# A split QKV projection on one core: a row tile of x loaded from ScalarE's queue, a block of w cut into slices, and a cast given to ScalarE

## The chip, the core and the metric

The kernel runs on one core of a Trainium2 chip. TensorE (PE) multiplies, VectorE (DVE), ScalarE (ACT) and GpSimd (POOL) cast, add and copy, and DMA queues that SyncE (SP) or ScalarE start move data between HBM and SBUF. The metric is the device time of one execution in microseconds; lower is better. Before the change it was 358.88 us, the median of 3 runs (358.77 to 358.99).

## The reference

```python
batch, seq, hidden = 16, 512, 768          # x (16, 512, 768), w_qkv (768, 2304), float32
qkv = np.matmul(x, w_qkv)
q, k, v = qkv[..., :768], qkv[..., 768:1536], qkv[..., 1536:]
return np.stack([q, k, v], axis=0).astype(np.float32)
```

So one matrix of 8192 x 768 is multiplied by one of 768 x 2304, and the result is stored as three matrices of 8192 x 768.

## The kernel before

**Tiling.** The 8192 rows of x are taken in 32 pairs of two row tiles of 128 rows. The contraction of 768 is cut into six steps j of 128. The 2304 columns of w are two groups of 1024 columns (q = 0 and q = 1 in the code, each of two blocks of 512, c = 0 and 1) and 256 remainder columns between them. From the third pair on (p = 2) a pair is multiplied by a group with a scheme of seven products instead of eight: `product` (L236) makes them from sums of row tiles (`sums_x`, L207) and sums of blocks of w (`sum_w`, L111, on VectorE). Two of the seven take bf16 copies (`xb`, `b1`), the other five take fp32r tiles (`s`, `t`, and `b22`, a copy of the lower half of block 1 that GpSimd makes). The remainder columns are multiplied plainly in bf16 (`rem`, L315, with the weights `w_rem0` and `w_rem1`).

**The start.** While w still arrives, pairs 0 and 1 are multiplied plainly with bf16 blocks (`block`, L468): block 0 of group 0 (24 matmuls, six steps j by four row tiles), then block 1 of group 0 (24 more), then the remainder columns of pairs 0 and 1 (24 matmuls of 256 columns, one `rem` per pair). Then comes the first product of pair 2 with group 0 (`do(u, 1)`, L580), and after it the third pair's other products are mixed with block work on group 1. After about 60 us the kernel is in a regular loop over pairs.

**The order is written out by hand.** `tc.manual_schedule()` keeps every engine's instructions in the order of the code, so one that waits holds all behind it on its engine. What matters here, by engine:

- SyncE's queue (L442 to L451): pair 0, pair 1, six slices of block 0, block 1 as two halves of three slices (0 to 2 and 3 to 5, 768 KB each), the remainder columns `str` (768 KB), pair 2 as eight DMAs of 96 KB (`load_x_rows`, four for each row tile), then the first block of group 1. Each DMA issue waits for the eighth DMA before it to have landed, since eight semaphores go round.
- VectorE (L547 to L563): cast of slice 0 and 2 of block 1, `sum_w(0, 1)`, cast of slice 4, `sum_w(0, 2)`, the cast into `w_rem0` (L558), then the two transposes of pair 2's row tiles (`transpose`, L155).
- ScalarE (L548 to L570): cast of slice 1, of 3 and of 5 of block 1, between and behind them the copies out of PSUM (`late0`, then `late`, L476), then `round_row(2, 0, act)` (L203), the bf16 copy of pair 2's first row tile that `do(u, 1)` multiplies.
- GpSimd (L559, L560): the cast into `w_rem1`, which waits for `str`; behind it the cast into `b22`, which reads slices 3 to 5 of block 1.

Of the kernel before, what the change touches and what calls it, by code (L numbers as in the profile page):

```python
# [10 lines left out]
def kernel(  # L11
# [20 lines left out]
    nc = tc.nc  # L32
    P = 128
    G = 32
# [4 lines left out]
    KT = K // P  # L39
    KH = KT // 2  # L40
    KC = K // 4
    NP = M // (2 * P)
    CB = 512
    REM = N3 - 4 * CB
    Q_OFF = (0, 2 * CB + REM)
    R_OFF = 2 * CB
    fp32 = mybir.dt.float32
    f32r = mybir.dt.float32r
    bf16 = mybir.dt.bfloat16
    ident = mybir.ActivationFunctionType.Identity  # L50
# [11 lines left out]
    o_pool = ctx.enter_context(tc.tile_pool(name="o", bufs=5))  # L62
# [13 lines left out]
    w_rem = [w_pool.tile([P, KH, REM], bf16, name="w_rem0"), None]  # L76
# [13 lines left out]
    def load_w(dst, j0, nj, off, cols):  # L90
        rows = w_qkv.rearrange("(p j) n -> p j n", j=KT)
        nc.sync.dma_start(dst, rows[:, j0:j0 + nj, off:off + cols])  # L92

    stage = {}

    def load_blocks(q, c, nj=KH):
        if q == 0:
            t = tq_pool.tile([P, KT, CB], fp32, name="st0", tag="tq")
            for j in range(0, KT, nj):
                load_w(t[:, j:j + nj], j, nj, Q_OFF[q] + c * CB, CB)  # L100
            stage[q, 0, c], stage[q, 1, c] = t[:, :KH, :], t[:, KH:, :]
        else:
            for h in range(2):
                if c == 0 and h == 0:
                    t = st_first
                else:
                    t = st_pool.tile([P, KH, CB], fp32, name="st1", tag="st")[:]
                load_w(t, h * KH, KH, Q_OFF[q] + c * CB, CB)
                stage[q, h, c] = t
# [11 lines left out]
    xin, xf, xb, sr = {}, {}, {}, {}  # L121
# [5 lines left out]
        for i in (2 * h, 2 * h + 1):  # L127
            eng.dma_start(xin[p][i * G:(i + 1) * G], rows[:, :, i * KC:(i + 1) * KC])

    def load_x_rows(p, parts=range(8)):  # L130
        if p not in xin:
            xin[p] = xin_pool.tile([P, 2 * P // G, KC], fp32, name="xin")
        rows = x_flat[p * 2 * P:(p + 1) * 2 * P, :].rearrange("(g b) k -> b g k", b=G)
        for n in parts:
            r, i = divmod(n, 4)
            gs = slice(r * P // G, (r + 1) * P // G)
            nc.sync.dma_start(  # L137
                xin[p][i * G:(i + 1) * G, gs], rows[:, gs, i * KC:(i + 1) * KC]
            )

# [18 lines left out]
    def load_rows(p):  # L159
        xin[p] = xin_pool.tile([P, 2, K], fp32, name="xin")  # L160
        rows = x_flat[p * 2 * P:(p + 1) * 2 * P, :]
        nc.sync.dma_start(xin[p][:], rows.rearrange("(r m) k -> m r k", m=P))  # L162
# [21 lines left out]
    def copy_row(p, r, h, eng):  # L184
        n = slice(h * KH, (h + 1) * KH)
        dst, src = xb[p][:, n, r * P:(r + 1) * P], turned_rows[p, r][:, n, :]
        if eng is nc.scalar:
            eng.activation(dst, src, ident)
        else:
            eng.tensor_copy(out=dst, in_=src)  # L190
# [5 lines left out]
    act, dve = nc.scalar, nc.vector  # L196
# [32 lines left out]
    def quad(p, q, pool=o_pool, tag="o"):  # L229
        u = Quad()  # L230
        u.p, u.q = p, q
        u.o = pool.tile([P, 2, 2 * CB], fp32, name="o", tag=tag)
        u.x = u.y = u.z = None
        return u
# [208 lines left out]
    nc.scalar.activation(tiny[:], zero[:, :1], ident)  # L443
    make_identity(nc, eye)
    load_rows(1)
    load_blocks(0, 0, 1)
    load_blocks(0, 1)
    st_rem = o_pool.tile([P, KT, REM], fp32, name="str", tag="o")
    load_w(st_rem[:], 0, KT, R_OFF, REM)
    load_x_rows(2)  # L450
    load_blocks(1, 0)  # L451

    def busy(n):

# [4 lines left out]
    def cast_j(q, c, w, j, eng=act):  # L459
        src = stage[q, j // KH, c][:, j % KH, :]  # L460
        if eng is act:
            eng.activation(w[:, j, :], src, ident)
        else:
            eng.tensor_copy(out=w[:, j, :], in_=src)
# [76 lines left out]
    shared_cast(b1[0][:, 1], stage[0, 0, 0][:, 1, :], 320)  # L541
    for p, r in ((0, 0), (0, 1), (1, 0), (1, 1)):
        copy_row(p, r, 1, act)
    for j in range(2, KT):
        cast_j(0, 0, b1[0], j, dve)
    late0 = block(0, 0, b1[0], singles)
# [9 lines left out]
    for f in late0[1:]:  # L556
        f()
    dve.tensor_copy(out=w_rem[0][:], in_=st_rem[:, :KH])  # L558
    nc.gpsimd.tensor_copy(out=w_rem[1][:], in_=st_rem[:, KH:])  # L559
    nc.gpsimd.tensor_copy(out=b22[0][:], in_=stage[0, 1, 1])  # L560
    late = block(0, 1, bt, [((j, ), range(4)) for j in range(KT)])
    rems = [rem(p) for p in range(2)]
# [20 lines left out]
    load_blocks(1, 1)  # L583
    for store in rem_stores:
        store()
    load_x_rows(3)
    for p in range(2):
        store_quad(quads[p, 0])
    load_x(4, nc.sync)
# [62 lines left out]
    for p in range(ND + 3, NP - 1, 2):  # L652
# [16 lines left out]
        c, d = quad(p + 1, 0), quad(p + 1, 1)  # L669
# [34 lines left out]
```

## Time and profile before

| what | value |
|---|---|
| median of 3 runs | 358.88 us (358.77 to 358.99) |
| the profiled execution's own time | 358.8 us |
| its span, first to last instruction | 357.0 us |
| TensorE busy | 350.5 us, 98% of the span |
| VectorE, ScalarE, GpSimd busy | 74%, 52%, 50% |
| DMA | 108.10 MB, mean 303 GB/s |
| granted TensorE clock | 1.000 |

A time in the profile is in us from the start of the span. A line of the timeline gives start, length, engine, source line, operation, the tile written and the tile read, their shapes and how many instructions are merged into the line; a bracket at its end says how long the engine sat idle before it and what ended that. A view by stretches gives, for each stretch of the span, the busy time of PE, PEld (weight loads), DVE, ACT and POOL, then the granted clock, the DMA engines' busy share and what they moved in GB/s. PE's matmuls are pipelined, so a start is a surer mark than an end, and a matmul that is listed with 379 ns may follow the one before it by far less.

### The profile page before, as it was taken

The page shows a single profiled execution, that of the slowest core. Times are in us where ns is not written, and L with a number is a line of the kernel's source. Part 1 is how long each engine was busy: PE and PEld are TensorE (multiplying, and loading weights), DVE is VectorE, ACT ScalarE, POOL GpSimd, SP SyncE. Part 2 cuts the span into 40 slices and gives each one's busy share as a digit, 9 for nine tenths or more (in the row PEclk, how much of TensorE's full clock was granted, in tenths as well). Part 3 has the DMA queues.
Part 4 walks back from the last instruction along what each step waited for, and adds up shares of the span by engine and source line. Part 5 has one row for each costly group of instructions (what it writes and reads, how often), then busy time and mean ns, then how long its engine had stood idle before and what let it go on. Part 6 is the DMA issues. An engine that isn't in the chain of part 4 may idle for free.

```text
span 357.0 us, 5317 instructions
## 1 busy us (share of the span) xinstructions
PE 350.5 (98%) x1757; PEld 252.0 (71%) x1776; DVE 264.5 (74%) x309; ACT 186.0 (52%) x320; POOL 177.6 (50%) x184
## 2 busy tenths in 40 slices
PE   8999999999999999999999999999999999999996
PEld 3464677768677686877768777686877768677674
DVE  3799876796877869777695877869777695876743
ACT  5588654545454553645545454553645545454553
POOL 0121774276566453665535566353665535566320
PEclk9999999999999999999999999999999999999999
DMA  7998999999999898999979899798999989896497
GB/s 301 375 351 273 322 369 356 381 302 372 259 345 310 256 355 206 355 258 299 352 188 388 226 328 320 237 376 213 347 263 308 329 213 376 231 328 249 155 376 264
DMA packets 82075, 108.10 MB, mean 303 GB/s; under 512 B 4992, under 2 KB 62080, under 8 KB 82048
## 3 DMA queue, kind: packets, MB, share of 16 engines
q1 hardware_dynamic: 75088, 102.52, 85.8%
q10 hardware_dynamic: 6960, 5.24, 5.6%
q8 instruction: 14, 0.23, 0.3%
q14 instruction: 13, 0.11, 0.1%
HBM read 32.24 MB, written 75.50 MB: 302 GB/s over the span
## 4 chain that ended last, share of the span: by engine, by line
PE 70%; POOL 15%; DVE 6%; DMA 4%; issue 3%; SPq 1%; ACT 0%; DVEq 0%
PE ps L247 56%; PE ps L310 11%; DVE xf L155 6%; POOL xb L194 5%; POOL s L215 3%; POOL s L214 3%; POOL s L216 3%; PE ps L484 3%; DMA xin<-in_x_dram 2%; DMA st<-in_w_qkv_dram 2%; SPq L137 1%; SPq L162 0%; ACT xb L203 0%; DVE o L293 0%; SPq L92 0%
## 5 line engine op out<-in xcount | busy, mean ns | idle before, releaser
L247 PE MATMUL ps<-t,s 128*128 128x512 f32 x720 | 177.9, 395 | 0.0
L247 PEld LDWEIGHTS ps<-t,s 128*128 128x128 f32 x720 | 135.0, 188 | 29.5
L155 DVE STREAM_TRANSPOSE xf<-xin 128x768 f32<-128x768 f32 (+1 forms) x45 | 93.3, 2075 | 2.2 <-DMA xin<-in_x_dram 2.2
L247 PE MATMUL ps<-b,xb 128*128 128x512 bf16 x343 | 81.5, 379 | 1.4 <-ACT xb L203 0.3
L287 DVE TENSOR_TENSOR o<-o,ps 128x512 f32<-128x512 f32 x56 | 38.5, 688 | 52.5 <-ACT o L286 52.5
L194 POOL CAST xb<-xf 128x1536 bf16<-128x1536 f32 x28 | 41.1, 1468 | 57.8 <-DVE xf L155 57.8
L214 POOL TENSOR_TENSOR s<-xf 128x384 fp32r<-128x384 f32 x29 | 31.0, 1069 | 72.1 <-DVE xf L155 70.3
L247 PEld LDWEIGHTS <-xb 128*128 128x128 bf16 x360 | 33.9, 98 | 37.0 <-issue 4.2
L293 DVE TENSOR_TENSOR o<-o,ps 128x512 f32<-128x512 f32 x60 | 41.1, 687 | 20.5 <-PE ps L247 19.4
L286 ACT ACTIVATE o<-ps 128x512 f32<-128x512 f32 x56 | 33.5, 598 | 42.0 <-PE ps L247 42.0
L247 PE MATMUL ps<-b,s 128*128 128x512 f32 x180 | 50.5, 389 | 0.0
L290 ACT ACTIVATE o<-ps 128x512 f32<-128x512 f32 x60 | 35.9, 599 | 25.2 <-PE ps L247 22.8
L367 DVE TENSOR_TENSOR o<-o,ps 128x512 f32<-128x512 f32 x78 | 47.8, 682 | 0.0
L310 PE MATMUL ps<-w_rem,xb 128*128 128x256 bf16 x384 | 47.3, 273 | 0.0
L275 ACT ACTIVATE o<-ps 128x512 f32<-128x512 f32 x60 | 36.0, 601 | 19.4 <-PE ps L247 14.1
L310 PEld LDWEIGHTS <-xb 128*128 128x128 bf16 x384 | 37.4, 98 | 11.4 <-issue 0.8
L324 ACT ACTIVATE orem<-ps 128x512 f32<-128x512 f32 x31 | 18.5, 597 | 47.6 <-PE ps L310 34.0
L247 PEld LDWEIGHTS ps<-b,s 128*128 128x128 f32 x180 | 33.8, 188 | 7.1
L215 POOL TENSOR_TENSOR s<-s,xf 128x384 fp32r<-128x384 f32 x29 | 29.6, 1021 | 2.3
L216 POOL TENSOR_TENSOR s<-xf 128x384 fp32r<-128x384 f32 x29 | 29.5, 1017 | 0.0
L218 POOL TENSOR_TENSOR s<-xf,s 128x384 fp32r<-128x384 f32 x29 | 29.4, 1012 | 0.0
L371 ACT ACTIVATE o<-ps 128x512 f32<-128x512 f32 x26 | 15.6, 599 | 17.8 <-PE ps L247 17.2
(51 smaller groups left out, 162.6 us busy)
## 6 DMA issues: line engine op xcount, KB each, us to landing
out_dram<-o SPq DMA_DIRECT2D x60, 768.0 KB, 4.6
out_dram<-o SPq DMA_DIRECT2D x75, 256.0 KB, 3.8
xin<-in_x_dram SPq DMA_DIRECT2D x88, 192.0 KB, 5.7
out_dram<-orem SPq DMA_DIRECT2D x31, 256.0 KB, 2.4
xin<-in_x_dram ACTq DMA_DIRECT2D x24, 192.0 KB, 4.1
st<-in_w_qkv_dram SPq DMA_DIRECT2D x5, 768.0 KB, 7.7
xin<-in_x_dram SPq DMA_DIRECT2D x2, 768.0 KB, 4.9
st<-in_w_qkv_dram SPq DMA_DIRECT2D x6, 256.0 KB, 5.9
```

The costliest lines, as they stand in the source:

```text
L155: nc.vector.transpose(turned[:, g:g + n], rows[:, g:g + n])
L194: nc.gpsimd.tensor_copy(out=xb[p][:], in_=xf[p][:])
L214: 1: lambda g: g.tensor_tensor(s[:, 1], a21, a22, op=add),
L215: 2: lambda g: g.tensor_tensor(s[:, 2], s[:, 1], a11, op=sub),
L216: 3: lambda g: g.tensor_tensor(s[:, 3], a11, a21, op=sub),
L247: nc.tensor.matmul(ps[:], lhs[j], rhs[j], start=(start and j == 0), stop=(j == KH - 1), skip_group_check=True,)
L275: nc.scalar.activation(c12, u.x[:], ident)
L287: nc.vector.tensor_tensor(c22, c22, u.y[:], op=add)
L290: nc.scalar.activation(c21, u.x[:], ident)
L293: nc.vector.tensor_tensor(c12, c12, u.y[:], op=add)
L310: nc.tensor.matmul(ps, xb[p][:, j, r * P:(r + 1) * P], w_rem[j // KH][:, j % KH, :], start=(j == 0), stop=(j == KT - 1), skip_group_check= ...
L367: dve.tensor_tensor(c, c, u.z[:], op=add)
```

## The change

Three things are done at once. First, pair 2's first row tile (four DMAs of 96 KB) is issued from ScalarE's queue instead of SyncE's, right behind the copies of pairs 0 and 1's transposed rows; on SyncE's queue the four for the second row tile stay, behind the remainder columns, and all x rows of a tile now go in the order 0, 2, 1, 3 of their quarters instead of 0, 1, 2, 3. Second, block 1 of group 0 is loaded as slices 0, 1 and 2 on their own and slices 3 to 5 together, instead of two halves of three. Third, the cast into `w_rem1` goes from GpSimd to ScalarE, where it stands behind the copies `late0` and before the copies `late`; GpSimd's first work is then the cast into `b22`.

```diff
-    def load_blocks(q, c, nj=KH):
+    def load_blocks(q, c, cuts=(0, KH, KT)):
         if q == 0:
             t = tq_pool.tile([P, KT, CB], fp32, name="st0", tag="tq")
-            for j in range(0, KT, nj):
-                load_w(t[:, j:j + nj], j, nj, Q_OFF[q] + c * CB, CB)
+            for j, end in zip(cuts, cuts[1:]):
+                load_w(t[:, j:end], j, end - j, Q_OFF[q] + c * CB, CB)
...
-    def load_x_rows(p, parts=range(8)):
-        if p not in xin:
+    def load_x_row(p, r, eng):
+        if r == 0:
             xin[p] = xin_pool.tile([P, 2 * P // G, KC], fp32, name="xin")
...
-        for n in parts:
-            r, i = divmod(n, 4)
-            gs = slice(r * P // G, (r + 1) * P // G)
-            nc.sync.dma_start(
+        gs = slice(r * P // G, (r + 1) * P // G)
+        for i in (0, 2, 1, 3):
+            eng.dma_start(
                 xin[p][i * G:(i + 1) * G, gs], rows[:, gs, i * KC:(i + 1) * KC]
             )
...
     load_rows(1)
-    load_blocks(0, 0, 1)
-    load_blocks(0, 1)
-    st_rem = o_pool.tile([P, KT, REM], fp32, name="str", tag="o")
-    load_w(st_rem[:], 0, KT, R_OFF, REM)
-    load_x_rows(2)
-    load_blocks(1, 0)
+    load_blocks(0, 0, range(KT + 1))
+    load_blocks(0, 1, (0, 1, 2, KH, KT))
...
     for p, r in ((0, 0), (0, 1), (1, 0), (1, 1)):
         copy_row(p, r, 1, act)
+    load_x_row(2, 0, nc.scalar)
+    st_rem = o_pool.tile([P, KT, REM], fp32, name="str", tag="o")
+    load_w(st_rem[:], 0, KT, R_OFF, REM)
+    load_x_row(2, 1, nc.sync)
+    load_blocks(1, 0)
...
     dve.tensor_copy(out=w_rem[0][:], in_=st_rem[:, :KH])
-    nc.gpsimd.tensor_copy(out=w_rem[1][:], in_=st_rem[:, KH:])
+    act.activation(w_rem[1][:], st_rem[:, KH:], ident)
     nc.gpsimd.tensor_copy(out=b22[0][:], in_=stage[0, 1, 1])
...
-    load_x_rows(3)
+    for r in range(2):
+        load_x_row(3, r, nc.sync)
```

## The prediction

> **What bounds the kernel now.** First the page's busy times and the waits of TensorE:
>
> ```profile
> PE 350.5 (98%) x1757; PEld 252.0 (71%) x1776; DVE 264.5 (74%) x309; ACT 186.0 (52%) x320; POOL 177.6 (50%) x184
> ```
> ```profile
> PE ps L181 <- ACT xc L168: 0.4, 1, 0.4
> PE ps L247 <- ACT xb L203: 0.3, 1, 0.3
> ```
>
> TensorE is the bound, and once real work starts (8.05 us) it waits once, for the bf16 copy of pair 2's first row tile. Its timeline and the chain of waits place that wait:
>
> ```profile
> 13.23 5.34 PE L484 MATMUL ps<-both,xb 128*128 128x512 bf16 x24
> 18.41 2.78 PE L310 MATMUL ps<-w_rem,xb 128*128 128x256 bf16 x24
> 21.52 1.24 PE L247 MATMUL ps<-b,xb 128*128 128x512 bf16 x5 [0.32 <-ACT xb L203]
> ```
> ```profile
> 11.37 7.27 DMA xin<-in_x_dram
> ...
> 18.77 1.60 DVE xf L155
> 20.39 0.85 ACT xb L203
> 21.24 0.27 issue
> 21.52 1.24 PE ps L247 x5
> ```
>
> From start to start, 24 matmuls of 512 columns take 18.41 - 13.23 = 5.18 us, 0.216 each; a step j of four takes 0.86. Twelve remainder matmuls take 1.31 by the chain, so 24 take 2.62, and TensorE could begin pair 2 at 21.03. It begins at 21.52, so 0.49 us is all this stall can give back, 0.14% of the run. The chain says why: the row's last DMA lands at 18.64, then transpose, copy and issue follow.
>
> Last, the engines beside it, and the queues:
>
> ```profile
> 15.00 0.42 DVE L464 CAST both<-st 128x512 bf16<-128x512 f32 x1
> 15.34 1.75 DVE L119 TENSOR_TENSOR t<-st,t 128x1536 fp32r<-128x1536 f32 x1
> 17.00 1.18 DVE L558 CAST w_rem<-str 128x768 bf16<-128x768 f32 x1
> ...
> 31.31 3.04 DVE L119 TENSOR_TENSOR t<-st,t 128x1536 fp32r<-128x1536 f32 x1 [0.20 <-DMA st<-in_w_qkv_dram]
> ```
> ```profile
> 16.94 0.83 POOL L559 CAST w_rem<-str 128x768 bf16<-128x768 f32 x1 [15.63 <-DMA str<-in_w_qkv_dram]
> 17.71 1.79 POOL L560 CAST b<-st 128x1536 fp32r<-128x1536 f32 x1
> 31.27 1.47 POOL L620 CAST b<-st 128x1536 fp32r<-128x1536 f32 x1 [8.31 <-DMA st<-in_w_qkv_dram]
> ```
> ```profile
> 14.54 1.15 ACT L462 ACTIVATE both<-st 128x512 bf16<-128x512 f32 x2 [0.77 <-DMA st<-in_w_qkv_dram]
> ```
> ```profile
> 10.00:15.00 5.00, 4.95 (x24) 2.29 (x24) 3.20 (x5) 1.76 (x4) 0.00 (x0) 1.00 1.05 401
> 120.00:121.50 1.50, 1.50 (x9) 0.75 (x7) 1.50 (x2) 0.39 (x1) 0.21 (x1) 1.00 1.09 334
> ```
> ```profile
> xin<-in_x_dram SPq DMA_DIRECT2D x88, 192.0 KB, 5.7
> xin<-in_x_dram ACTq DMA_DIRECT2D x24, 192.0 KB, 4.1
> ```
>
> The reader should see four things. The DMA engines are full while w arrives (401 GB/s at a share of 1.05). Slices 3 to 5 of block 1 land at 14.52 (ACT starts on them at 14.54), 1.3 us before TensorE needs slice 3 (13.23 + 3 x 0.86 = 15.82). A sum of w on VectorE takes 1.75 us alone and 3.04 when GpSimd began its 1.47 us cast of the same block 0.04 us earlier: 1.29 lost. In group 0 the same two never met, as GpSimd's cast into b22 stood behind the cast into w_rem1, which waited for the remainder columns until 16.94.
>
> **The change, part by part.**
>
> *Row tile on ScalarE's queue.* ScalarE's last copy of the transposed rows starts at 9.67 and ends at 10.19, so the four DMAs go out from about 9.7, at 0.32 to 0.52 each (two take 0.86 to 0.90 in the loop). In the changed program the fourth waits for slice 0 of block 1 (about 11.4); behind it stands the cast of slice 1, which lands about 12.0 and isn't needed until 14.09, so this costs ScalarE nothing; were that DMA stuck beyond 13.4, it would cost one for one. On the wire it costs. The second half of block 1 is queued until 13.5 or so, and the rows come from another queue, whose loads overtake: 4.1 us to landing against 5.7 on SyncE's. 393 KB must pass while w is under way. At 334 GB/s (the stretch at 120 us, two x streams side by side) that is 1.18 us; at the pace of the eight DMAs before, which landed within 16.89 to 20.16, 3.27 / 8 = 0.41 each, 1.64; if SyncE's packets all went first, 0. I take 1.18, being nearest to two queues at once. A gain for w is excluded, as the engines are full.
>
> *Slices 0 to 2 singly.* Single slices land 0.65 us apart (7.43, 8.13, 8.77), three make 1.95 against 1.89 for a half: 0.06 more. The casts of slices 0 and 2 may start earlier, but TensorE didn't wait at 13.23: 0 gained. The cover is block 0's matmuls; without it an earlier slice 0 would be worth up to 1.2. So slices 3 to 5 land at 14.52 + 0.06 + 1.18 = 15.75 (bounds 14.58 and 16.2).
>
> *Remainder columns later.* Their 16.89 becomes 18.1 by the same 1.24. The second row tile follows within 1.64, at the latest 19.8, and its transpose needs it after 21: 0. All x rows and the block behind them are as many bytes as before: 0, and what lies behind lands no later.
>
> *Slice 3.* ScalarE casts it in 0.63: 15.75 + 0.63 + 0.05 = 16.43, so TensorE, ready at 15.82, stands 0.6.
>
> *GpSimd freed of the w_rem1 cast.* The cast into b22 now waits for slices 3 to 5 alone, as VectorE's cast of slice 4 does. Whoever comes first, VectorE must get a cast (0.43) and `sum_w(0, 2)` (1.75) done and GpSimd 1.47 in the same time, and the row at 31.31 shows that they exclude each other. Then comes the cast into w_rem0: 288 columns take 0.31 and 512 take 0.43, so 768 take 0.56 with GpSimd idle, against 1.18 beside GpSimd's cast. End: 15.75 + 0.05 + 0.43 + 1.47 + 1.75 + 0.56 = 20.0. Bounds of the exclusion: 0, and 1.47; I take 1.47, near the 1.29 seen. If slice 4's cast is the one held, TensorE stands 0.3 more there, inside the next wait.
>
> *w_rem1 on ScalarE.* Slices 3 and 5 end at 17.0, the three late0 copies at 18.5 (1.55), the cast takes 0.85 as row L203 of that size does: 19.4, before TensorE is there. Cost 0; the cover is VectorE's later w_rem0. Behind it, two PSUM copies (1.08) end at 20.5, before the row copy.
>
> *Sum.* The remainder matmuls start at 20.05 instead of 18.41 and end at 22.67. The row tile's own path is 20.0 + 1.60 + 0.02 + 0.85 + 0.27 = 22.74. So pair 2 starts at 22.7 instead of 21.52: its wait is gone, and two or three new ones ahead of it are worth more. Later work is as dense as before, with VectorE shifted alike, so 1.2 us reaches the end. The profiled execution took 358.8 (357.0 span and 1.8 around it), 0.08 under the median: 358.8 + 1.2 = 360.0.
>
> Two rules bear on this. The Trainium skill ("DMA: Bandwidth & Descriptors", Queues, rings and completion order) says each DMA engine takes turns between queues packet by packet, and "Issuing engines are not separate DMA queues" that a second engine saves only issue time: by that rule the rows do cost w their full share, and the sum stands at 360.0. No row here shows such a turn packet by packet. "SBUF — State Buffer" (SBUF: two separate sides) in the Trainium skill says that of GpSimd and such a VectorE operation the first to start holds the port for its whole length: by that the loss would be 1.47 in any order, against 1.29 in the row.
>
> **Rivals.**
>
> *No meeting of VectorE and GpSimd.* If VectorE keeps its turn through cast and sum, w_rem0 is cast at 18.1 and ready by 18.7; TensorE, late by 0.6 through slice 3, starts the remainder at 19.05 and pair 2 at 21.67: +0.15, 358.95. For it: at 22.09 a GpSimd cast took 0.87 instead of 0.50 beside VectorE, so VectorE wins at times. Against: at 16.94 and at 31.27 GpSimd started first on a shared landing.
>
> *Not slower: w is not delayed.* If SyncE's packets go first, slices 3 to 5 land at 14.58; with the b22 meeting w_rem0 is ready at 18.85 and pair 2 starts at 21.6: +0.1, 358.9. Without the meeting TensorE runs through and gains the whole stall: -0.49, 358.3. It decides if the half lands before 15.27 (less than 0.72 us lost). Against it: the 4.1 us of ScalarE's loads.
>
> *More.* At 1.64 for the rows the half lands at 16.2 and all moves 0.46 further: +1.65, 360.5. For it: the old pace was just that; against: the new order of quarters and the mix with w.
>
> **Chances.** A measurement of this kernel tells no less than about 0.2%, 0.72 us, from no change. The forecast, 0.75 to 1.45 us longer (359.5 to 360.3), 0.58; more than that 0.13; no meeting 0.15; w not delayed 0.09, with the full gain of 0.49 us another 0.03; a gain over 0.72, for which no wait is there, 0.02. The first two are slower, 0.71; the next three within 0.2%, 0.27. From 358.9 to 360.7 leaves out the gains and part of the undelayed case below and the tail above, about 0.15.
>
> **What would show it.** The four issues on ScalarE from 9.7; ScalarE's cast of slice 3 near 15.8 instead of 14.54; GpSimd's b22 cast starting with it; VectorE's slice-4 cast or its next sum stretched by 1 us or more; TensorE idle before slice 3, perhaps slice 4, and before the first remainder matmul near 20; pair 2 at 22.7. I am wrong if the half still lands before 15.3, if cast and sum run at 0.43 and 1.75, or if TensorE shows no gap between 13 and 20.

## The result, and the profile after

The changed kernel takes 360.61 us (median of 6 runs, 360.58 to 360.74) against 358.77 for the kernel before beside it (6 runs, 358.67 to 358.99): 1.84 us slower, a ratio of 1.0049 with a 95% interval of 1.0039 to 1.0059. The forecast was slower, 360.0, with a range of 358.9 to 360.7.

The page of the changed kernel, its busy line, shows the same work as before; its waits of TensorE (time in total, times, longest) show that the old wait for pair 2's bf16 copy is gone and two new ones stand in its place. The page counts a wait from the modelled end of the matmul before it, so it gives a little less than the starts below do.

```profile
PE 350.7 (98%) x1757; PEld 252.2 (70%) x1776; DVE 263.7 (74%) x309; ACT 187.3 (52%) x321; POOL 176.7 (49%) x183
```
```profile
PE ps L479 <- ACT both L457: 1.1, 1, 1.1
...
PE ps L309 <- DVE w_rem L558: 0.5, 1, 0.5
```

TensorE's timeline of the changed kernel puts them before slice 3 of block 1 and before the first remainder matmul:

```profile
13.27 2.75 PE L479 MATMUL ps<-both,xb 128*128 128x512 bf16 x12
17.11 2.75 PE L479 MATMUL ps<-both,xb 128*128 128x512 bf16 x12 [1.08 <-ACT both L457]
20.31 2.78 PE L309 MATMUL ps<-w_rem,xb 128*128 128x256 bf16 x24 [0.45 <-DVE w_rem L558]
23.14 1.24 PE L246 MATMUL ps<-b,xb 128*128 128x512 bf16 x5
```

Twelve matmuls at 0.216 us take 2.59, so slice 3 was due at 13.27 + 2.59 = 15.86 and began at 17.11, 1.25 later; the remainder was due at 17.11 + 2.59 = 19.70 and began at 20.31, 0.61 later. The chain of waits (start, length, what) goes through the load of slices 3 to 5, VectorE's cast, its sum and the cast into w_rem0, where before it went through the x rows:

```profile
8.82 7.58 DMA st<-in_w_qkv_dram
...
16.43 0.43 DVE both L459
16.86 2.06 DVE t L119
...
19.71 0.37 DVE w_rem L558
```

On VectorE and GpSimd of the changed kernel the sum and the cast into b22 now fall together:

```profile
16.43 0.43 DVE L459 CAST both<-st 128x512 bf16<-128x512 f32 x1 [1.32 <-DMA st<-in_w_qkv_dram]
16.77 3.02 DVE L119 TENSOR_TENSOR t<-st,t 128x1536 fp32r<-128x1536 f32 x1
19.71 0.55 DVE L558 CAST w_rem<-str 128x768 bf16<-128x768 f32 x1
```
```profile
16.46 1.72 POOL L560 CAST b<-st 128x1536 fp32r<-128x1536 f32 x1 [15.15 <-DMA st<-in_w_qkv_dram]
```

The same 21 matmuls near the end, before and after, show that the delay reaches the end whole:

```profile
345.85 5.12 PE L247 MATMUL ps<-t,s 128*128 128x512 f32 x21
```
```profile
347.48 5.12 PE L246 MATMUL ps<-t,s 128*128 128x512 f32 x21
```

That is 1.63 us, all of it lost in the first 21 us. The span grew by 1.8 (357.0 to 358.8), the time by 1.84. The rest lies behind the last matmul: the last store lands 1.67 later (356.18 to 357.85), and from that landing to the end of the span it took 0.84 us before and 0.94 after. The last 0.1 goes with the slices: of the kernels below, the six that load block 1 in slices show 0.94 there and the five with halves 0.83 or 0.84. Why is not shown.

### The profile page after: what moved, and what is told of

Read it like the earlier page. It is cut to its first block, busy times and chain, and to the rows that moved or that the text cites. A ratio compares the mean times of both kernels' runs of the same rounds, so it can differ in the third digit from the quotient of the medians.

```text
span 358.8 us, 5318 instructions
## 1 busy us (share of the span) xinstructions
PE 350.7 (98%) x1757; PEld 252.2 (70%) x1776; DVE 263.7 (74%) x309; ACT 187.3 (52%) x321; POOL 176.7 (49%) x183
## 4 chain that ended last, share of the span: by engine, by line
PE 70%; POOL 15%; DVE 7%; DMA 4%; issue 3%; SPq 1%; ACT 0%; DVEq 0%
PE ps L246 56%; PE ps L309 11%; DVE xf L154 6%; POOL xb L193 5%; DMA st<-in_w_qkv_dram 4%; POOL s L214 3%; POOL s L213 3%; POOL s L215 3%; PE ps L479 3%; DVE t L119 1%; SPq L92 0%; SPq L161 0%; ACT xb L202 0%; DVE o L292 0%; ACT orem L323 0%
## 5 line engine op out<-in xcount | busy, mean ns | idle before, releaser
L323 ACT ACTIVATE orem<-ps 128x512 f32<-128x512 f32 x31 | 18.5, 596 | 46.8 <-PE ps L309 33.3
L370 ACT ACTIVATE o<-ps 128x512 f32<-128x512 f32 x26 | 15.5, 598 | 17.4 <-PE ps L246 16.7
```

## The experiments

The theory after the result: the x rows on ScalarE's queue hold back slices 3 to 5 of w; TensorE pays once before slice 3; and GpSimd's cast into b22, freed of the wait for the remainder columns, meets VectorE's sum and makes TensorE pay again before the remainder matmuls. The rivals: the cast moved to ScalarE costs nothing by itself or all of it; the slices are neutral; two queues at once are themselves slow. Each time stands against the kernel before in the same round; the traces are one execution each.

The table holds what was read from each run's timeline: when ScalarE starts its cast of slice 3 (within 0.03 us of the landing of slices 3 to 5), how long `sum_w(0, 2)` takes on VectorE, when the remainder matmuls start, and the median times, with the kernel before beside it.

| kernel | slice 3 cast | sum | remainder | time | before |
|---|---|---|---|---|---|
| before | 14.54 | 1.75 | 18.41 | | 358.77 |
| whole change | 16.43 | 3.02 | 20.31 | 360.61 | 358.77 |
| rows alone | 15.78 | 1.75 | 19.20 | 359.70 | 358.81 |
| cast alone | 14.61 | 1.75 | 18.94 | 359.09 | 358.81 |
| slices alone | 14.66 | 1.75 | 18.47 | 358.82 | 358.69 |
| rows and slices | 16.37 | 1.75 | 19.64 | 359.93 | 358.69 |
| rows and cast | 15.78 | 3.02 | 19.66 | 359.80 | 358.69 |
| whole, b22 late | 16.27 | 1.75 | 19.53 | 360.21 | 358.81 |
| whole, rows ahead on SyncE | 16.25 | 3.02 | 20.14 | 360.60 | 358.81 |
| whole, rows issued later | 14.65 | 3.02 | 18.56 | 359.31 | 358.81 |
| before, order of quarters | 14.63 | 1.75 | 18.51 | 358.58 | 358.69 |

### The row tile's loads alone

Against the changed kernel:

```diff
-    load_blocks(0, 1, (0, 1, 2, KH, KT))
+    load_blocks(0, 1)
...
-    act.activation(w_rem[1][:], st_rem[:, KH:], ident)
+    nc.gpsimd.tensor_copy(out=w_rem[1][:], in_=st_rem[:, KH:])
```

> Only the first row tile's loads move to ScalarE's queue; block 1 of w comes in two halves and the cast into w_rem1 stays on GpSimd, as before the change. Theory (the rows delay w by their bytes): slices 3 to 5 again land near 16.4 instead of 14.5, TensorE stands about 1.2 us before slice 3; the sum of w then runs at 1.75 us, but the cast into w_rem0 meets GpSimd's cast into w_rem1 and takes about 1.2 instead of 0.55, so the remainder matmuls start near 20.2 and the time is 360.4 to 360.6, as with the whole change. Rival (the meeting of GpSimd's b22 cast with the sum is a cost of its own, added by the moved cast): remainder matmuls start at 19.7 and the time is about 360.0 or less.

Measured: 359.70 us, ratio 1.0022 (1.0013 to 1.0032). The theory's forecast missed; the rival's time held (360.0 or less), though the remainder matmuls began earlier than its 19.7. Slices 3 to 5 landed near 15.8, not 16.4, so the stall before slice 3 was shorter; and in the meeting of the two remainder casts it was GpSimd's that gave way (1.21 us instead of 0.83), not VectorE's. VectorE, GpSimd, then TensorE:

```profile
15.78 0.43 DVE L459 CAST both<-st 128x512 bf16<-128x512 f32 x1 [0.69 <-DMA st<-in_w_qkv_dram]
16.12 1.75 DVE L119 TENSOR_TENSOR t<-st,t 128x1536 fp32r<-128x1536 f32 x1
18.59 0.56 DVE L558 CAST w_rem<-str 128x768 bf16<-128x768 f32 x1 [0.71 <-DMA str<-in_w_qkv_dram]
```
```profile
18.62 1.21 POOL L559 CAST w_rem<-str 128x768 bf16<-128x768 f32 x1 [17.31 <-DMA str<-in_w_qkv_dram]
19.77 1.46 POOL L560 CAST b<-st 128x1536 fp32r<-128x1536 f32 x1
```
```profile
16.46 2.75 PE L479 MATMUL ps<-both,xb 128*128 128x512 bf16 x12 [0.44 <-ACT both L457]
19.20 0.49 PE L309 MATMUL ps<-w_rem,xb 128*128 128x256 bf16 x3
19.88 2.45 PE L309 MATMUL ps<-w_rem,xb 128*128 128x256 bf16 x21 [0.19 <-POOL w_rem L559]
22.17 1.46 PE L246 MATMUL ps<-b,xb 128*128 128x512 bf16 x6
```

So the rows alone cost 0.9 us. TensorE loses 0.60 before slice 3 (16.46 instead of 15.86). It loses 0.15 more before the remainder matmuls (19.20 instead of 16.46 + 2.59 = 19.05), since the remainder columns landed at 18.6 instead of 16.9. And it loses 0.35 inside them, waiting for GpSimd's cast into w_rem1: pair 2 begins at 22.17, not at 19.20 + 2.62 = 21.82. The old wait before pair 2 is gone in return. That left 0.9 of the 1.84 to the other two parts, and raised the question of why slices 3 to 5 were 0.65 later in the whole change.

### The cast alone

Against the kernel before:

```diff
-    nc.gpsimd.tensor_copy(out=w_rem[1][:], in_=st_rem[:, KH:])
+    act.activation(w_rem[1][:], st_rem[:, KH:], ident)
```

> Only the cast into w_rem1 moves from GpSimd to ScalarE; all loads are as before the change. Theory (GpSimd's cast into b22, no longer held back by the remainder columns, meets VectorE's cast and sum even when w is on time): b22 starts at 14.5 to 15.1, the sum or the cast in front of it is stretched by about 1.3 us, w_rem0 is ready near 18.9 to 19.2, and the kernel is 0.3 to 0.6 us slower than before, 359.1 to 359.4. Rival (without the late rows there is no meeting): the cast into w_rem0 takes 0.55 instead of 1.18 us and the time is that of before, 358.8.

Measured: 359.09 us, ratio 1.0006 (0.9997 to 1.0016); the step of 0.28 us is at the lower end of the theory's range, and the interval doesn't exclude none. The timeline does: with every load as before, GpSimd starts b22 at 14.63, VectorE's cast of slice 4 takes 1.68 us instead of 0.42, and TensorE waits 0.25 for w_rem0.

```profile
15.06 1.68 DVE L464 CAST both<-st 128x512 bf16<-128x512 f32 x1
16.67 1.75 DVE L119 TENSOR_TENSOR t<-st,t 128x1536 fp32r<-128x1536 f32 x1
18.34 0.55 DVE L558 CAST w_rem<-str 128x768 bf16<-128x768 f32 x1
```
```profile
14.63 1.83 POOL L560 CAST b<-st 128x1536 fp32r<-128x1536 f32 x1 [13.33 <-DMA st<-in_w_qkv_dram]
```
```profile
18.94 2.78 PE L310 MATMUL ps<-w_rem,xb 128*128 128x256 bf16 x24 [0.25 <-DVE w_rem L558]
```

### The whole change without the meeting

Against the changed kernel:

```diff
-    nc.gpsimd.tensor_copy(out=b22[0][:], in_=stage[0, 1, 1])
...
     sums[0](nc.gpsimd)
+    nc.gpsimd.tensor_copy(out=b22[0][:], in_=stage[0, 1, 1])
```

> The whole change, but GpSimd makes b22 only after its copy for the sums of pair 2 (about 24 us), so it cannot meet the sum of w in block 1. Theory: slices 3 to 5 land at 16.4 and TensorE stands 1.25 us before slice 3 as with the change, the sum takes 1.75 instead of 3.02 us, the gap of 0.6 us before the remainder matmuls is gone, and the kernel is 0.6 us faster than the changed one: 360.0. Rival (the remainder columns' landing at 18.9 sets the remainder matmuls): no gain, 360.6. Second rival (the cast now meets later sums and TensorE pays there): 360.6 or more.

Measured: 360.21 us in the median, but its runs spread from 359.88 to 360.72, so the time alone doesn't show the step of 0.6. The timeline, taken of the fastest of the four runs, does: the sum takes 1.75 us, and the remainder matmuls follow slice 5 without a gap.

```profile
16.95 2.75 PE L479 MATMUL ps<-both,xb 128*128 128x512 bf16 x12 [0.95 <-ACT both L457]
19.53 2.78 PE L309 MATMUL ps<-w_rem,xb 128*128 128x256 bf16 x24
22.15 1.46 PE L246 MATMUL ps<-b,xb 128*128 128x512 bf16 x6
```

Pair 2 begins 0.78 before the changed kernel's (22.15 against 22.93; the changed kernel's list lacks the first of its six matmuls). Slices 3 to 5 landed 0.16 earlier here, so 0.62 are the meeting's, which is the 0.61 that the changed kernel lost before its remainder matmuls. A later sum, which b22 met instead, took 3.01 us, and the page shows no wait of TensorE for it; its last matmul ends 0.94 later than before where pair 2 began 0.85 later, so it cost TensorE no more than 0.1.

### One queue for everything

Against the changed kernel:

```diff
-    load_blocks(0, 1, (0, 1, 2, KH, KT))
+    for j in range(KH):
+        load_w(t01[:, j:j + 1], j, 1, Q_OFF[0] + CB, CB)
+    load_x_row(2, 0, nc.sync)
+    load_w(t01[:, KH:], KH, KH, Q_OFF[0] + CB, CB)
...
-    load_x_row(2, 0, nc.scalar)
```

> The whole change, but the first row tile's four loads go out from SyncE, between slice 2 and slices 3 to 5 of block 1, so that one queue carries everything. Theory (what the rows cost w is the time their own transfers take, about 0.45 us for each 96 KB, whatever the queue): slices 3 to 5 land at 16.2 to 16.5 and the time is 360.5 to 360.7. Rival (taking turns between two queues is itself slow): they land at 15.6 to 16.0 and the time is 359.8 to 360.3.

Measured: 360.60 us (four runs, 360.39 to 361.13), ratio 1.0054 (1.0038 to 1.0071), as the theory said. With the rows put outright ahead of slices 3 to 5 on SyncE's queue, these land at 16.23 and the time is that of the changed kernel within the spread of the runs. The Trainium skill ("DMA: Bandwidth & Descriptors", Issuing engines are not separate DMA queues) says a second issuing engine saves only issue time; 360.60 against 360.61 agrees. The stretch from 12.5 to 15.5 us has in its last column 394 GB/s in the kernel before, 326 in the changed one and 347 with one queue, in this order:

```profile
12.50:15.50 3.00, 3.00 (x16) 1.37 (x14) 2.85 (x5) 2.07 (x4) 0.00 (x0) 1.00 1.06 394
```
```profile
12.50:15.50 3.00, 3.00 (x16) 1.35 (x15) 2.10 (x2) 0.74 (x2) 0.00 (x0) 1.00 1.07 326
```
```profile
12.50:15.50 3.00, 3.00 (x16) 1.35 (x15) 2.10 (x2) 0.74 (x2) 0.00 (x0) 1.00 1.07 347
```

The rows take time out of proportion to their bytes on one queue as on two: 393 KB at 394 GB/s would be 1.0 us, and put outright ahead they held slices 3 to 5 back by 1.6 (16.23 against 14.64 in the kernel with the slices alone). With two queues these slices landed 0.17 later still (16.41); that is one trace of each, and the times don't tell the two apart.

### Rows with slices, rows with the cast, slices alone

Against the changed kernel, the first two:

```diff
     # rows and slices: the whole change without the cast
-    act.activation(w_rem[1][:], st_rem[:, KH:], ident)
+    nc.gpsimd.tensor_copy(out=w_rem[1][:], in_=st_rem[:, KH:])
```

> The row tile on ScalarE's queue and block 1 in slices, the cast into w_rem1 left on GpSimd. Theory (the slices cost nothing by themselves, but they put the issue of slices 3 to 5 behind the first x load, so the rows pass more of them): slices 3 to 5 land at 16.2 to 16.5 as with the whole change, against 15.8 with the rows alone; TensorE stands about 1.2 us before slice 3, the sum of w takes 1.75 us, and the time is 360.0 to 360.3. Rival (the slices are neutral): they land at 15.8 and the time is that of the rows alone, 359.7.

```diff
     # rows and cast: the whole change without the slices
-    load_blocks(0, 1, (0, 1, 2, KH, KT))
+    load_blocks(0, 1)
```

> The row tile on ScalarE's queue and the w_rem1 cast on ScalarE, block 1 of w in two halves. Theory: slices 3 to 5 land at 15.8 as with the rows alone, and GpSimd's b22 cast stretches the cast or the sum behind it by 1.3 us, so the cast into w_rem0 ends near 19.5 to 19.7 instead of 19.1 and the remainder matmuls start 0.5 to 0.7 us later than with the rows alone: 360.1 to 360.3. Rival (the meeting costs no more here than with the cast alone, 0.3 us): 360.0 or less.

```diff
     # slices alone: the kernel before with
-    load_blocks(0, 1)
+    load_blocks(0, 1, (0, 1, 2, KH, KT))
```

> Only block 1 of w as slices 0, 1, 2 and 3 to 5; all else as before the change. Theory: no row stands between them, slices 3 to 5 land within 0.1 us of 14.5, nothing waits for slice 0 earlier, and the time is that of before, 358.7 to 358.9. Rival (smaller loads cost w by themselves): slices 3 to 5 land at 15 or later and the time is 359.0 or more.

Measured: 359.93 (ratio 1.0033, 1.0020 to 1.0047), 359.80 (1.0030, 1.0019 to 1.0042) and 358.82 (1.0005, 0.9996 to 1.0014). Slices alone are neutral in time: TensorE's last matmul ends 0.14 earlier than before, and the longer stretch behind it takes that back. With the rows they bring slices 3 to 5 from 15.76 to 16.35, as the theory said. 359.93 lies just below the 360.0 to 360.3 that it gave: TensorE starts slice 3 at 17.05 and the remainder matmuls right behind slice 5 (17.05 + 2.59 = 19.64), with no second wait.

```profile
17.05 2.75 PE L479 MATMUL ps<-both,xb 128*128 128x512 bf16 x12 [0.96 <-ACT both L457]
19.64 2.81 PE L309 MATMUL ps<-w_rem,xb 128*128 128x256 bf16 x24
```

Rows and cast miss the theory's 360.1 to 360.3 in the rival's favour. The sum is stretched to 3.02 and the remainder matmuls start at 19.66, 0.46 after those of the rows alone. But there TensorE lost 0.35 inside them to GpSimd's cast into w_rem1, and here that cast is ScalarE's: pair 2 begins at 22.27 (19.66 + 2.62), only 0.1 after the 22.17 of the rows alone.

```profile
16.12 3.02 DVE L119 TENSOR_TENSOR t<-st,t 128x1536 fp32r<-128x1536 f32 x1
19.06 0.55 DVE L558 CAST w_rem<-str 128x768 bf16<-128x768 f32 x1
```

So the parts don't add. From the landing of slices 3 to 5 the stretched sum needs 3.9 us to the remainder matmuls (15.76 to 19.66, 16.23 to 20.14, 16.41 to 20.31), and the unstretched one no more than the 3.3 that TensorE itself needs from the same landing (16.35 to 19.64, 16.24 to 19.53). Either the rows with slices or the rows with the cast cost 1.1 to 1.2; the three together 1.84, since a late landing and a long chain from it come one after the other.

### The rows issued later

Against the changed kernel:

```diff
-    load_x_row(2, 0, nc.scalar)
...
     cast_j(0, 1, bt, 1, act)
+    load_x_row(2, 0, nc.scalar)
```

The lines of SyncE's loads behind the remainder columns move down with it; their order stays.

> The whole change, but ScalarE issues the row tile's four loads behind its cast of slice 1 (about 12 us) instead of 8.7 to 11.4, so all of slices 3 to 5 is queued before them. Theory (what a load passes on the other queue depends on which was issued first; in the changed kernel the first x load went out at 8.69, just ahead of slices 3 to 5 at 8.83): slices 3 to 5 land at 14.6 to 15.0 instead of 16.4, TensorE hardly stands before slice 3, the remainder columns' landing near 18.5 and the meeting of b22 with VectorE then set the remainder matmuls at 18.9 to 19.3, and the time is 359.1 to 359.4. Rival (two queues share whatever the order of issue): they land at 15.6 or later and the time is 359.8 or more.

Measured: 359.31 us, ratio 1.0013 (1.0004 to 1.0023). Slices 3 to 5 land at 14.63, as if no rows were on the other queue (14.64 with the slices alone). The order of issue alone, which the theory went by, doesn't explain it: with the rows alone slices 3 to 5 were issued at 7.49, 1.2 us ahead of the first row load, and still landed 1.24 late (15.76 against 14.52 before); and here the remainder columns, issued at 9.44, landed behind the first row load that went out at 12.03 (17.53 against 17.26). In these kernels the first row load landed 4.8 to 5.6 us after its issue (8.69 to 13.52, 8.68 to 14.29, 12.03 to 17.26), so the rows held back what was still under way by then; how the two queues take turns on the way is not shown. TensorE stands nowhere before the remainder matmuls, although b22 meets the sum; it now waits for the row tile again, which lands at 19.07:

```profile
13.28 5.34 PE L479 MATMUL ps<-both,xb 128*128 128x512 bf16 x24
18.56 2.78 PE L309 MATMUL ps<-w_rem,xb 128*128 128x256 bf16 x24
21.81 1.24 PE L246 MATMUL ps<-b,xb 128*128 128x512 bf16 x5 [0.47 <-ACT xb L202]
```

The time was in the theory's range with one part of its reasoning wrong: the remainder columns landed at 17.5, not 18.5, and were not what TensorE waited for.

### The order of the quarters alone

Against the kernel before:

```diff
-            r, i = divmod(n, 4)
+            r, i = n // 4, (0, 2, 1, 3)[n % 4]
```

> The kernel before with one thing changed: the four loads of each row tile go out in the order 0, 2, 1, 3 of their quarters of the partitions, still from SyncE behind the remainder columns. Theory (each quarter of 32 partitions is written at a pace that two loads to different halves of the partitions share better): the first row tile lands 0.2 to 0.4 us earlier than 18.64, the wait before pair 2 (0.27 us by its weight loads) shrinks or goes, and the time is 358.5 to 358.7. Rival (the order doesn't matter): 358.8.

Measured: 358.58 us against 358.69, ratio 0.9997 (0.9988 to 1.0006): in the range of the theory, and not resolved by the runs from no change. The trace is clearer. The first row tile lands at 18.17, 0.47 earlier and not 0.2 to 0.4. From the first to the last of the eight row loads the landings took 2.32 us (17.17 to 19.49) instead of 2.77 (17.39 to 20.17), the transposes begin 0.48 earlier than 18.77, and TensorE waits nowhere after its first matmul on w:

```profile
18.29 3.06 DVE L155 STREAM_TRANSPOSE xf<-xin 128x768 f32<-128x768 f32 x2
```
```profile
18.51 2.78 PE L310 MATMUL ps<-w_rem,xb 128*128 128x256 bf16 x24
21.35 1.24 PE L247 MATMUL ps<-b,xb 128*128 128x512 bf16 x5
```

## Why the prediction was right, step by step

**Direction and mechanism.** It named both new waits, their places and the engines in them, and both were there. It was 0.6 us short of the time: 1.84 us lies in the stated range but above the 0.75 to 1.45 that it held likeliest, in the "more than that" to which it gave 0.13. Three terms were off, and one of them the other way.

**Slices 3 to 5 land at 15.75.** They landed at 16.41 (ScalarE's cast at 16.43). This is the term mis-sized, 0.66 us. Two steps of its working failed. "The four DMAs go out from about 9.7" was wrong: the first went out at 8.69, before ScalarE's earlier copies had run, as its timeline shows:

```profile
8.60 0.48 ACT L187 ACTIVATE xb<-ps 128x384 bf16<-128x384 bf16 x1
8.69 0.48 ACTq L136 DMA_DIRECT2D xin<-in_x_dram  x1
8.97 0.87 ACT L187 ACTIVATE xb<-ps 128x384 bf16<-128x384 bf16 x2
9.43 0.32 ACTq L136 DMA_DIRECT2D xin<-in_x_dram  x1
9.71 0.51 ACT L187 ACTIVATE xb<-ps 128x384 bf16<-128x384 bf16 x1
```

That step by itself did not move the landing: with the rows alone the first load went out just as early (8.68), and slices 3 to 5 landed at 15.76, the figure worked out. What moved it was the other step, "0.06 more" for slices 0 to 2 singly, which is near the truth only without the rows (14.64 against 14.52). With two more loads in the round of eight semaphores, the load of slices 3 to 5 waited for slice 2 of block 0 (8.81) and went out at 8.82, behind the first row load, instead of 7.49 with the halves; the rows then cost it 0.65 more. That 15.76 agrees with the figure worked out is luck: the figure takes 1.18 us for all four loads at 334 GB/s, and only two of the four had landed by then (14.29 and 15.22, then 16.00 and 16.72). Four loads put ahead outright cost 16.23 - 14.64 = 1.6, near the upper bound's 1.64.

**Slice 3: 0.6.** It was 1.25, by the same 0.66.

**The meeting: 1.47.** It took 3.02 - 1.75 = 1.27, and the cast of slice 4 came first at 0.43, so TensorE did not stand before slice 4. VectorE's cast ran to 16.86, GpSimd then until 16.46 + 1.72 = 18.18, and the sum ended at 19.79, 1.6 after that, where alone it takes 1.75. The Trainium skill ("SBUF — State Buffer", SBUF: two separate sides) says that the first to start holds the shared port for its whole length and the other is blocked fully; this trace agrees, 3.02 against 1.75. The whole chain from the landing to TensorE came to 3.9 us where 4.3 was worked out, which took 0.4 back.

**w_rem0 in 0.56, w_rem1 hidden, the remainder columns in time.** 0.55; ScalarE's cast ran from 18.91 to 19.76, under the wait for w_rem0; the columns landed at 18.86, later than the 18.1 worked out and still before VectorE was free at 19.7.

**Pair 2 at 22.7 instead of 21.52.** By the list it is 23.14. But both lists lack the first of the six matmuls (x5), and the weight load of the first began at 21.28 before, so the true starts are about 21.30 and 22.93. The old wait was 0.27 us and not 0.49, as the page's "0.3" that the prediction shows beside it had said: the gain that the change could have brought was little more than half of what the prediction granted it. So pair 2 began 0.23 later than worked out (22.93 against 22.7) and, before the change, 0.22 earlier than read (21.30 against 21.52); with the 1.18 between 21.52 and 22.7 that makes the 1.63 seen on TensorE.

**To the end whole.** Right: 1.63 at 347 us as at 23.

**The rivals.** The one without a meeting falls by the sum's 3.02. One of its reasons against it was misread: at 16.94 GpSimd didn't win a shared landing, since VectorE was still in its sum (15.34 + 1.75 = 17.09). The one with w undelayed is what the run with the later issue shows, and there pair 2 begins at 21.59, where the rival had 21.6, later than the 21.30 of before. The one with a slower pace of the rows, 360.5, was nearest in time and in the landing of slices 3 to 5 (16.2).

## What to carry to other kernels

Where the DMA engines are full, moving a load to a second queue is choosing what to delay: ask which transfers will still be under way when it comes through, how much slack their readers have, and note that cutting other loads into more pieces shifts their issue when semaphores go round. A wait can be a useful order: GpSimd's cast was kept away from VectorE's sum only by standing behind another wait, and taking that away made two independent instructions collide. Before pricing a stall, set the weight loads beside the matmuls, since one missing record nearly doubled this one.

## What the runs showed of the hardware that I had not expected

A DMA issue on ScalarE's queue ran up to 1.0 us ahead of copies that stand before it in the program (issues at 8.69 and 9.43, the last copy at 9.71). So the written order, which keeps a waiting instruction ahead of all behind it on its engine, did not make these issues wait for the copies to run. Loads of 96 KB to a quarter of the partitions took 0.40 us each in the order 0, 1, 2, 3 (2.77 us for seven steps) and 0.33 in the order 0, 2, 1, 3 (2.32), while 256 KB slices to all partitions took 0.65. In six other kernels with the second order, the four loads of the second row tile came 0.34 to 0.41 apart, 0.41 with the rows alone; so that the pace is set by which partitions are written is argued from this, not shown. And when GpSimd and VectorE woke on the same landing, either could be first: VectorE by 0.03 us at 18.59 with the rows alone (GpSimd's cast took 1.21 instead of 0.83), GpSimd by 0.04 us at 31.27 in the kernel before (VectorE's sum took 3.04 instead of 1.75).
